# Row gathers without pacing marks in a hybrid decoder block with product-key experts

## The chip, the cores and the metric

One core of a Trainium2 chip runs the whole block in one launch. The metric is device time in microseconds (us) of one execution; the time of a kernel is the median of its runs.

## The reference

The block takes 512 tokens of width 2048. A normalised copy goes through a gated causal convolution and a grouped diagonal state-space model, both are gated, summed, projected and added to the input. Then comes the expert layer, where the stretch of this case lies. In the reference:

```python
s_top, i_top = lax.top_k(s, PEER_TOPK)                 # 8 heads, 2 halves, 128 keys each
best, pos = lax.top_k(cand, PEER_TOPK)                 # cand: sums of pairs
gates = jax.nn.softmax(best, axis=-1)
u_sel, v_sel = u_tab[expert], v_tab[expert]            # tables of 16384 x 2048
act = jax.nn.gelu(jnp.einsum('td,thkd->thk', xb, u_sel))
return jnp.einsum('thk,thkd->td', gates * act, v_sel)
```

So each token takes 8 x 16 = 128 rows of `peer_u`, forms 128 dot products, and adds 128 weighted rows of `peer_v`. A last norm gives the output. All is float32.

## The kernel before

**Two ways through the experts.** Tokens 160 to 511 (352 of them, `ND`) are done densely: all 16384 experts are multiplied on TensorE and the unchosen are masked by a gate of zero. Tokens 0 to 159 (`G0`: a block of `GA` = 128 and one of `GB` = 32) are done by gathering the chosen rows from the tables. The two run side by side in the last 2160 us.

**The dense way.** The 16384 experts are 128 blocks j of 128. `dense_u(j)` multiplies the tokens by one block of `peer_u` (48 matmuls) and applies gelu on ScalarE, which gives `ga`. `weigh(j, ga)` multiplies `ga` by the gates of the block on VectorE (line 987; the gates of `QG` = 4 blocks come in one tile `gq`, which has a single buffer, loaded by `load_gates` on the GpSimd queue) and splits the result in a high part `wh` (ScalarE, line 209) and a low part `wl` (VectorE, line 210). `dense_v(g, dc, ws)` multiplies eight such blocks, group g, by a quarter dc of the columns of `peer_v` (96 matmuls) and adds the result to `acc` on VectorE (`_add`, line 61).

**The loop.** For every group g (16) and quarter dc (4): two new blocks jn go through `dense_u` and `weigh` (from block `LEAD` = 32 on; the first 32 were computed earlier and are read back as `gar`), then `dense_v`. I call one pass of this inner loop a quarter. Quarters of g = 0 to 2 have `dense_v` alone (96 matmuls), those of g = 3 to 14, 48 of them, have all of it (192 matmuls), those of g = 15 have `dense_v` alone again.

**Weights.** Weights are float32 and are used as a high and a low part. `Stream` loads pieces of 512 KB (`wraw`, SyncE's queue), ScalarE makes `whi`, VectorE makes `wlo` (`split`, lines 209 and 210). A piece feeds 24 matmuls; six pieces may be on the way, three of them split. There are four buffers of each part, so the part of a piece can be made once the matmuls of the piece four before it are done, about three pieces ahead of its use. In a quarter of 192 matmuls eight pieces are split.

**The gathered way.** `gather()` is a generator. A step takes one expert for each of 128 partitions: `gather_row` has GpSimd start an indirect DMA of 128 rows of 8 KB (1 MB, tile `grow`), and VectorE does one pass of 128x2048 over it, a dot product for `peer_u` (line 1113) or a weighted sum for `peer_v` (line 1116). There are three buffers (`NROW`), and a gather into a buffer waits for the pass that read it last, three steps before. The steps are 128 + 128 for the first block of tokens and 32 + 32 for the second. `pump_rows(n)` advances the generator; in a full quarter it is called four times with `rate / 2`, after each `weigh`, before and after `dense_v`: 6.1 steps in a quarter.

**Order.** Each engine has one queue and works it in order. A planner lays out the queues when the program is built: it follows the order of the program, but may put an instruction ahead of others that by its own estimate are not ready yet. `with after(x)` ties the instructions of its block on the engine of x behind x in that queue; it adds no wait. In the kernel before, `paced(ap)` has GpSimd copy one column of a tile just made (`ga`, or `acc` after `dense_v`) into a small tile `mark`, and every gather started by `gather_row` is tied behind the latest mark.

Of the kernel before, what the change touches and what calls it, by code (L numbers as in the profile page):

```python
# [7 lines left out]
F32 = mybir.dt.float32  # L8
# [25 lines left out]
NE = 128  # L34
# [121 lines left out]
def kernel(ctx, tc, xT, vecs, cst, w_in, conv_w_out, w_vg, w_out, w_q, keysT,  # L156
# [47 lines left out]
        return pp.tile([128, T], F32, name="ps", tag="proj", bufs=4)  # L204

    pace = [None]

    def split(hi, lo, src, eng=None):
        ins = nc.scalar.copy(hi, src).ins  # L209
        low = (eng or nc.vector).tensor_tensor(lo, src, hi.bitcast(F32), op=ALU.subtract)  # L210
        if eng is nc.gpsimd:
            pace[0] = low.ins
        return ins

    rings = {"raw": [(wp, 4)], "hi": [(wp, 3)], "lo": [(wp, 3)]}
# [763 lines left out]

    def weigh(j, ga):  # L980

        if j % QG == 0:
            load_gates(j // QG)
        if j < LEAD:
            ga = gars.pop(j) if j in gars else reload(j)
        g3 = ga.rearrange("p (b t) -> p b t", t=32)
        nc.vector.tensor_tensor(g3, gq[0][:, :, j % QG, :], g3, op=ALU.mult)  # L987
        p = wgp[j // GRP % 2]
        wh, wl = (p.tile([128, ND], F32R, name=n, tag="w") for n in ("wh", "wl"))
        split(wh, wl, ga)  # L990
        return wh, wl

    def reload(j):
# [60 lines left out]

    def gather_row(tab, ids, e):
        g = row("grow")
        with after(pace[0]):
            nc.gpsimd.indirect_dma_start(out=g, out_offset=None, in_=tab,
                                         in_offset=bass.IndirectOffsetOnAxis(ap=ids[:, e:e + 1], axis=0))
        return g  # L1060

    def gather():
        blocks = [(0, GA, eidx, gta, HK, rt[:, 0:1]),
                  (GA, GB, eidb, gtb, HK // REP, rtb)]
        passes = [(b, tab) for b in blocks for tab in (peer_u, peer_v)]
        todo = [(tab, b[2], e) for b, tab in passes for e in range(b[4])]
        live, xt, gain = [], [], []

        def ahead():
            if todo:  # L1070
                live.append(gather_row(*todo.pop(0)))

        def load(b):
            t0, n = b[:2]
            x = row("xt")
            for c in range(128 // n):
                nc.sync.dma_start(x[c * n:(c + 1) * n], d_xr[t0:t0 + n])
            xt.append(x)

        def load_gain():  # L1080
            gain.append(row("gain"))
            nc.gpsimd.dma_start(gain[0], gffn[None, :].to_broadcast([128, D]))

        def turn(scale):
            x2 = rowp.tile([128, D], F32, name="rows0", tag="rows", bufs=1)
            nc.scalar.activation(x2, xt.pop(), AF.Copy, scale=scale)
            return x2

        load(blocks[0])
        load_gain()  # L1090
        for _ in range(3):
            yield
        for p, (b, tab) in enumerate(passes):
            t0, n, ids, gates, steps, r = b
            nxt = passes[p + 1] if p + 1 < len(passes) else (None, None)
            if tab is peer_u:
                x = turn(r)
                ahead()
                _mul(nc, x, x, gain.pop())
            else:  # L1100
                x = turn(float(n) / 128)
            while len(live) < 2:
                ahead()
            for i in range(steps):
                if i == steps - 2 and nxt[0]:
                    load(nxt[0])
                elif i == steps - 1 and nxt[1] is peer_u:
                    load_gain()
                else:
                    ahead()  # L1110
                g = live.pop(0)
                if tab is peer_u:
                    nc.vector.scalar_tensor_tensor(g, g, 1.0, x, op0=ALU.mult, op1=ALU.mult,  # L1113
                                                   accum_out=act[:, i:i + 1])
                else:
                    nc.vector.scalar_tensor_tensor(x, g, act[:, i:i + 1], x, op0=ALU.mult, op1=ALU.add)  # L1116
                yield
            if tab is peer_u:
                with after(last_ga[0]):
                    nc.scalar.activation(act[:, :steps], act[:, :steps], AF.Gelu_apprx_tanh)  # L1120
                _mul(nc, act[:, :steps], act[:, :steps], gates)
                continue
            if n < 128:
                for _ in range(3):
                    yield
                y = row("ysum")
                for q in range(4):
                    pt = ps_v()
                    nc.tensor.matmul(pt[:n], sel, x[:, q * 512:(q + 1) * 512], start=True, stop=True)  # L1129
                    nc.scalar.copy(y[:n, q * 512:(q + 1) * 512], pt[:n])  # L1130
                x = y
            nc.sync.dma_start(out[t0:t0 + n, :], row_norm(x[:n], gfin))
        yield
# [2 lines left out]
    gth = gather()  # L1136
    gi = [0, 0.0]

    def paced(ap):

        mark = con2.tile([128, 1], F32, name="mark", tag="mark", bufs=2)
        pace[0] = nc.gpsimd.tensor_copy(mark, ap[:, 0:1]).ins  # L1142

    def pump_rows(n):
        gi[1] += n
        while gi[0] < gi[1]:
# [4 lines left out]
    for j in range(LEAD):  # L1151
        if j >= LEAD - 4:
            jn = 2 * (j - LEAD + 4)
            gars.update((i, reload(i)) for i in (jn, jn + 1))
        if j == 0:
            rows_load()
        if j in (4, 6):
            rows_turn()
        ga = dense_u(j, gate_steps if j >= LAG else None)
        if j == LAG - 1:  # L1160
            transp_routes()
        if j >= LEAD - 5:
            paced(ga)
            pump_rows(RLEAD)
        if j >= LEAD - 4:
            ws_next += [weigh(jn, None), weigh(jn + 1, None)]
# [50 lines left out]
    def dense_v(g, dc, ws):  # L1217
        pcs = []
        pairs = [ps_v((2, 512)) for _ in range(2)]
        pvs = [pairs[i // 2][:, i % 2, :ND] for i in range(4)]  # L1220
        last = range(GRP - 2, GRP)
        order = [(e, i) for e in range(GRP - 2) for i in range(4)] + [(e, i) for i in range(4) for e in last]
        for at, (e, i) in enumerate(order):
            if at == 16 and g == NE // GRP - 1 and dc:
                turn_out(dc - 1)
            if e // 2 == len(pcs):
                pcs.append(tabs.take())
            hi, lo = pcs[e // 2]
            wh, wl = ws[e]
            s = slice(e % 2 * 512 + i * 128, e % 2 * 512 + (i + 1) * 128)  # L1230
            nc.tensor.matmul(pvs[i], hi[:, s], wh, start=e == 0, stop=False)  # L1231
            nc.tensor.matmul(pvs[i], hi[:, s], wl, start=False, stop=False)  # L1232
            nc.tensor.matmul(pvs[i], lo[:, s], wh, start=False, stop=e == GRP - 1)  # L1233
        for h in range(2):
            a, pv = acc[:, 4 * dc + 2 * h:4 * dc + 2 * h + 2], pairs[h][:, :, :ND]
            _add(nc, a, pv, a if g else res[dc][:, 2 * h:2 * h + 2])
        paced(acc[:, 4 * dc + 3])
        if g == NE // GRP - 1 and dc == 3:
            turn_out(dc)

# [2 lines left out]
    for g in range(ngrp):  # L1243
        ws = ws_next
        ws_next = []
        for dc in range(4):
            if g == ngrp - 1 and dc == 3:
                for _ in gth:
                    pass
            if g == ngrp - 1 and dc == 0:  # L1250
                hst.close()
                op = ctx.enter_context(tc.tile_pool(name="op", bufs=1, reuse_waits="tile"))
                tail["ost"] = op.tile([128, len(BLKS), D], F32, name="ost")
                tail["sqs"] = op.tile([128, len(BLKS), 4], F32, name="sqs")
                tail["gfb"] = op.tile([128, D], F32, name="gfb")
                nc.gpsimd.dma_start(tail["gfb"], gfin[None, :].to_broadcast([128, D]))
            for jn in range((g + 1) * GRP + 2 * dc, (g + 1) * GRP + 2 * dc + 2):
                if jn < NE:
                    ga = None
                    if jn >= LEAD:  # L1260
                        ga = dense_u(jn)
                        paced(ga)
                    ws_next.append(weigh(jn, ga))
                    if jn >= LEAD:
                        pump_rows(rate / 2)
            n = RV / 4 * (3 + (g > 0)) if (g + 1) * GRP < LEAD else rate / 2 if g < ngrp - 1 else REND / 2 if dc < 3 else 0
            if g == 0 and dc < 3:
                load_res()
            pump_rows(n)
            dense_v(g, dc, ws)  # L1270
            pump_rows(n)
# [83 lines left out]
```

## Time and profile before

| what | value |
| --- | --- |
| median of 3 runs | 3835.49 us (3828.89 to 3838.25) |
| the profiled execution's own time | 3822.91 us |
| its span, from the first to the last instruction | 3821.1 us |
| mean granted TensorE clock | 0.959 |
| TensorE busy with matmuls | 3514.3 us, 92% |
| VectorE busy | 2712.8 us, 71% |
| ScalarE busy | 1256.4 us, 33% |
| GpSimd busy | 1004.8 us, 26% |
| moved by DMA | 852.35 MB, mean 223 GB/s |

The busy shares are means over the whole span, whose stages differ: up to about 1480 us the projections, convolution, state space and routing run, then the first 32 blocks of `dense_u`, and from 1661 us the loop. PEclk is the clock that TensorE was granted as a share of full speed. A DMA share is the mean busy share of the core's 16 DMA engines. Idle time is put down to the engine or transfer whose signal ended it.

### The profile page before, as it was taken

The page shows a single profiled execution, that of the slowest core. Times are in us where ns is not written, and L with a number is a line of the kernel's source. Part 1 is how long each engine was busy: PE and PEld are TensorE (multiplying, and loading weights), DVE is VectorE, ACT ScalarE, POOL GpSimd, SP SyncE. Part 2 cuts the span into 40 slices and gives each one's busy share as a digit, 9 for nine tenths or more (in the row PEclk, how much of TensorE's full clock was granted, in tenths as well). Part 3 has the DMA queues.
Part 4 walks back from the last instruction along what each step waited for, and adds up shares of the span by engine and source line. Part 5 has one row for each costly group of instructions (what it writes and reads, how often), then busy time and mean ns, then how long its engine had stood idle before and what let it go on. Part 6 is the DMA issues. An engine that isn't in the chain of part 4 may idle for free. (4 is left out here: it accounts for less than half of the span.)

```text
span 3821.1 us, 49889 instructions
## 1 busy us (share of the span) xinstructions
PE 3514.3 (92%) x19059; PEld 3257.5 (85%) x19059; DVE 2712.8 (71%) x4006; ACT 1256.4 (33%) x2009; POOL 1004.8 (26%) x832
## 2 busy tenths in 40 slices
PE   8999999999999999989998998988788888889877
PEld 6888888888888899988998998888788887889877
DVE  8686678985349998756667677676576666767666
ACT  4334434242323348732222222232222222232223
POOL 1100001000025452121233233333343333332331
PEclk9999999999999999999999999999899999999988
DMA  5533444344444356687678888886788767888874
GB/s 184 140 109 115 127 126 143 114 133 140 141 136 121 116 165 208 224 304 254 236 289 301 302 304 306 302 305 245 262 299 292 283 248 267 300 303 308 313 274 182
DMA packets 218863, 852.35 MB, mean 223 GB/s; under 512 B 41168, under 2 KB 58656, under 8 KB 173376
## 3 DMA queue, kind: packets, MB, share of 16 engines
q1 hardware_dynamic: 144704, 437.58, 35.8%
q0 software_dynamic: 64512, 396.12, 27.3%
q10 hardware_dynamic: 9408, 15.47, 1.1%
q8 instruction: 149, 2.44, 0.3%
q14 instruction: 90, 0.74, 0.1%
HBM read 795.23 MB, written 53.84 MB: 222 GB/s over the span
## 5 line engine op out<-in xcount | busy, mean ns | idle before, releaser
L209 ACT CAST whi<-wraw 128x1024 fp32r<-128x1024 f32 x736 | 761.6, 1049 | 1462.4 <-PE ps L269 575.0
L210 DVE TENSOR_TENSOR wlo<-wraw,whi 128x1024 fp32r<-128x1024 f32 x682 | 830.6, 1225 | 227.1 <-ACT whi L209 226.7
L1233 PE MATMUL pv<-wh,wlo 128*128 128x352 f32 x2048 | 707.2, 345 | 178.3 <-DVE wlo L210 178.2
L1231 PE MATMUL pv<-wh,whi 128*128 128x352 f32 x2048 | 704.4, 344 | 34.8 <-DVE acc L61 32.8
L270 PE MATMUL pu<-h2h,wlo 128*128 128x352 f32 x2048 | 676.0, 330 | 50.8 <-DVE wlo L210 50.8
L1232 PE MATMUL pv<-wl,whi 128*128 128x352 f32 x2048 | 696.5, 340 | 0.0
L268 PE MATMUL pu<-h2l,whi 128*128 128x352 f32 x2048 | 681.1, 333 | 1.1 <-ACT whi L209 1.1
L269 PE MATMUL pu<-h2h,whi 128*128 128x352 f32 x2048 | 668.2, 326 | 0.0
L1116 DVE SCALAR_TENSOR_TENSOR rows<-grow,act,rows 128x2048 f32<-128x2048 f32 x160 | 375.7, 2348 | 332.2 <-DMA grow<-in_peer_v_dram,eidx 282.1
L1233 PEld LDWEIGHTS pv<-wh,wlo 128*128 128x128 f32 x2048 | 417.8, 204 | 194.3 <-DVE wlo L210 194.3
L1113 DVE SCALAR_TENSOR_TENSOR grow<-grow,rows 128x2048 f32<-128x2048 f32 x160 | 366.2, 2289 | 277.3 <-DMA grow<-in_peer_u_dram,eidx 227.4
L1231 PEld LDWEIGHTS pv<-wh,whi 128*128 128x128 f32 x2048 | 418.3, 204 | 39.2 <-DVE acc L61 36.0
L270 PEld LDWEIGHTS pu<-h2h,wlo 128*128 128x128 f32 x2048 | 390.7, 191 | 58.1 <-DVE wlo L210 58.0
L1232 PEld LDWEIGHTS pv<-wl,whi 128*128 128x128 f32 x2048 | 419.0, 205 | 0.0
L268 PEld LDWEIGHTS pu<-h2l,whi 128*128 128x128 f32 x2048 | 393.3, 192 | 1.4 <-ACT whi L209 1.4
L269 PEld LDWEIGHTS pu<-h2h,whi 128*128 128x128 f32 x2048 | 391.8, 191 | 0.0
L268 PE MATMUL ps<-hl,whi 128*128 128x512 f32 x896 | 353.2, 394 | 8.7 <-ACT whi L209 8.7
L270 PE MATMUL ps<-hh,wlo 128*128 128x512 f32 x896 | 350.7, 392 | 0.5 <-DVE wlo L210 0.4
L269 PE MATMUL ps<-hh,whi 128*128 128x512 f32 x896 | 350.2, 391 | 0.0
L209 ACT CAST wh<-ga 128x352 fp32r<-128x352 f32 x96 | 46.7, 486 | 834.7 <-DVE ga L987 834.7
L1142 POOL COPY mark<-acc 128x1 f32<-128x1 f32 x64 | 84.5, 1320 | 757.2 <-DVE acc L61 757.2
L1142 POOL COPY mark<-ga 128x1 f32<-128x1 f32 x101 | 97.5, 966 | 506.5 <-ACT ga L916 492.4
(347 smaller groups left out, 5134.0 us busy)
## 6 DMA issues: line engine op xcount, KB each, us to landing
wraw<-in_peer_ut_dram SPq DMA_DIRECT2D x256, 512.0 KB
wraw<-in_peer_vt_dram SPq DMA_DIRECT2D x256, 512.0 KB
wraw<-in_w_in_dram SPq DMA_DIRECT2D x112, 512.0 KB
d_g<-stg SPq DMA_DIRECT2D x22, 1024.0 KB
gq<-d_g POOLq DMA_DIRECT2D x32, 704.0 KB, 11.1
wraw<-in_w_vg_dram SPq DMA_DIRECT2D x32, 512.0 KB
wraw<-in_w_out_dram SPq DMA_DIRECT2D x32, 512.0 KB
wraw<-in_w_q_dram SPq DMA_DIRECT2D x32, 512.0 KB
```

The costliest lines, as they stand in the source:

```text
L209: ins = nc.scalar.copy(hi, src).ins
L210: low = (eng or nc.vector).tensor_tensor(lo, src, hi.bitcast(F32), op=ALU.subtract)
L268: nc.tensor.matmul(ps, hi[:, sl], al[k], start=k == 0, stop=False)
L269: nc.tensor.matmul(ps, hi[:, sl], ah[k], start=False, stop=False)
L270: nc.tensor.matmul(ps, lo[:, sl], ah[k], start=False, stop=k == nk - 1)
L1113: nc.vector.scalar_tensor_tensor(g, g, 1.0, x, op0=ALU.mult, op1=ALU.mult, accum_out=act[:, i:i + 1])
L1116: nc.vector.scalar_tensor_tensor(x, g, act[:, i:i + 1], x, op0=ALU.mult, op1=ALU.add)
L1142: pace[0] = nc.gpsimd.tensor_copy(mark, ap[:, 0:1]).ins
L1231: nc.tensor.matmul(pvs[i], hi[:, s], wh, start=e == 0, stop=False)
L1232: nc.tensor.matmul(pvs[i], hi[:, s], wl, start=False, stop=False)
L1233: nc.tensor.matmul(pvs[i], lo[:, s], wh, start=False, stop=e == GRP - 1)
```

## The change

Three edits. The marks go, with `paced`, and the gathers are no longer tied to anything: each waits only for its buffer and its indices. VectorE's pass over a row is tied behind the low part that VectorE was last given in the order of the program (`last_low`, kept by `split`). And the gates of a group of four blocks are loaded after the last block of the group before has been weighed, rather than just ahead of their first use.

```diff
+    last_low = [None]
...
         if eng is nc.gpsimd:
             pace[0] = low.ins
+        else:
+            last_low[0] = low.ins
...
-        if j % QG == 0:
-            load_gates(j // QG)
+        if j == 0:
+            load_gates(0)
...
         split(wh, wl, ga)
+        if j % QG == QG - 1 and j + 1 < NE:
+            load_gates(j // QG + 1)
...
         g = row("grow")
-        with after(pace[0]):
-            nc.gpsimd.indirect_dma_start(out=g, out_offset=None, in_=tab,
-                                         in_offset=bass.IndirectOffsetOnAxis(ap=ids[:, e:e + 1], axis=0))
+        nc.gpsimd.indirect_dma_start(out=g, out_offset=None, in_=tab,
+                                     in_offset=bass.IndirectOffsetOnAxis(ap=ids[:, e:e + 1], axis=0))
...
-                if tab is peer_u:
-                    nc.vector.scalar_tensor_tensor(g, g, 1.0, x, op0=ALU.mult, op1=ALU.mult,
-                                                   accum_out=act[:, i:i + 1])
-                else:
-                    nc.vector.scalar_tensor_tensor(x, g, act[:, i:i + 1], x, op0=ALU.mult, op1=ALU.add)
+                with after(last_low[0]):
+                    if tab is peer_u:
+                        nc.vector.scalar_tensor_tensor(g, g, 1.0, x, op0=ALU.mult, op1=ALU.mult,
+                                                       accum_out=act[:, i:i + 1])
+                    else:
+                        nc.vector.scalar_tensor_tensor(x, g, act[:, i:i + 1], x, op0=ALU.mult, op1=ALU.add)
...
-    def paced(ap):
-
-        mark = con2.tile([128, 1], F32, name="mark", tag="mark", bufs=2)
-        pace[0] = nc.gpsimd.tensor_copy(mark, ap[:, 0:1]).ins
...
         if j >= LEAD - 5:
-            paced(ga)
             pump_rows(RLEAD)
...
-        paced(acc[:, 4 * dc + 3])
...
                         ga = dense_u(jn)
-                        paced(ga)
                     ws_next.append(weigh(jn, ga))
```

## Rows read from the trace of the kernel before

**Rows 1.** The page: busy time, share of the span, instructions.
```profile
PE   3514.3 (92%) x19059; PEld 3257.5 (85%) x19059; DVE 2712.8 (71%) x4006; ACT 1256.4 (33%) x2009; POOL 1004.8 (26%) x832
```

**Rows 2.** Waits from 1886.9 to 3712 us: total, times, longest.
```profile
DVE rows L1116 <- DMA grow<-in_peer_v_dram,eidx: 282.1, 47, 9.9
...
PE pv L1233 <- DVE wlo L210: 177.1, 51, 6.2
...
DVE grow L1113 <- DMA grow<-in_peer_u_dram,eidx: 187.7, 46, 9.6
...
PE pu L270 <- DVE wlo L210: 46.5, 22, 5.4
```

**Rows 3.** Stages and single quarters: engines' busy time (instructions), clock, DMA share, GB/s.
```profile
1660.90:1886.90 226.00, 200.87 (x1155) 196.93 (x1155) 145.36 (x165) 63.95 (x78) 39.92 (x38) 0.94 0.77 267
1886.90:1917.80 30.90, 30.90 (x193) 30.90 (x192) 20.88 (x21) 9.73 (x13) 13.12 (x9) 1.00 0.83 305
2063.60:2101.00 37.40, 33.54 (x194) 33.26 (x193) 27.58 (x30) 9.69 (x13) 11.90 (x10) 0.91 0.75 285
1886.90:3712.00 1825.10, 1601.48 (x9217) 1579.75 (x9216) 1256.10 (x1107) 474.69 (x587) 628.63 (x461) 0.93 0.80 290
3712.00:3821.00 109.00, 76.34 (x441) 71.23 (x439) 68.26 (x83) 31.61 (x54) 19.26 (x15) 0.87 0.51 192
...
1799.20:1814.70 15.50, 15.50 (x98) 15.50 (x97) 10.05 (x11) 5.93 (x9) 3.27 (x3) 1.00 0.87 308
```

**Rows 4.** VectorE's timeline in one quarter: start, duration, instruction, idle before.
```profile
2061.53 2.29 DVE L1113 SCALAR_TENSOR_TENSOR grow<-grow,rows 128x2048 f32<-128x2048 f32 x1 [1.91 <-DMA grow<-in_peer_u_dram,eidx]
...
2069.60 2.29 DVE L1113 SCALAR_TENSOR_TENSOR grow<-grow,rows 128x2048 f32<-128x2048 f32 x1
...
2083.33 2.29 DVE L1113 SCALAR_TENSOR_TENSOR grow<-grow,rows 128x2048 f32<-128x2048 f32 x1 [8.36 <-DMA grow<-in_peer_u_dram,eidx]
...
2085.98 1.22 DVE L210 TENSOR_TENSOR wlo<-wraw,whi 128x1024 fp32r<-128x1024 f32 x1
```

**Rows 5.** GpSimd's timeline in the same quarter.
```profile
2072.84 1.04 POOL L1142 COPY mark<-acc 128x1 f32<-128x1 f32 x1 [12.40 <-DVE acc L61]
2074.03 1.77 POOL L1058 DMA_INDIRECT grow<-in_peer_u_dram,eidx  x1 [0.16 <-issue]
...
2077.41 0.97 POOL L1058 DMA_INDIRECT grow<-in_peer_u_dram,eidx  x1 [0.15 <-issue]
```

**Rows 6.** TensorE's timeline in the same quarter.
```profile
2087.26 0.66 PE L1233 MATMUL pv<-wh,wlo 128*128 128x352 f32 x1 [3.86 <-DVE wlo L210]
```

**Rows 7.** Line 1058: issue time on GpSimd (ns min/median/max), issue to landing.
```profile
L1058 POOL DMA_INDIRECT grow<-in_peer_v_dram,eidx x128: 941/970/4914, 2547.5 to 3364.6; - x128
...
DMA to landing us min/median/max: 5.3/9.4/15.1
```

**Rows 8.** Around 3405 to 3433 us: GpSimd, VectorE, then two stretches.
```profile
3413.46 1.71 POOL L1058 DMA_INDIRECT grow<-in_peer_u_dram,eidb  x1 [2.63 <-DVE grow L1113]
...
3421.51 2.29 DVE L1113 SCALAR_TENSOR_TENSOR grow<-grow,rows 128x2048 f32<-128x2048 f32 x1 [0.75 <-DMA grow<-in_peer_u_dram,eidb]
...
3400.00:3500.00 100.00, 91.46 (x542) 89.54 (x541) 78.66 (x79) 28.71 (x36) 35.58 (x30) 0.97 0.90 336
...
3405.00:3433.00 28.00, 23.72 (x142) 22.56 (x142) 24.80 (x23) 5.80 (x7) 12.67 (x10) 1.00 1.00 379
```

**Rows 9.** Waits from 1660.9 to 1886.9 us.
```profile
PE pv L1231 <- DVE acc L61: 22.0, 9, 4.2
...
DVE gar L987 <- DMA gq<-d_g: 8.3, 3, 5.4
```

**Rows 10.** Waits from 3712 us to the end.
```profile
DVE rows L1116 <- DMA grow<-in_peer_v_dram,eidb: 15.5, 5, 7.6
...
PE pv L1231 <- DVE acc L61: 10.9, 2, 9.6
...
PE pv L1201 <- DVE acc L61: 7.4, 2, 6.7
```

## The prediction

> **What bounds the kernel now.** I read the busy shares first: TensorE is busy 92% of the span and VectorE 71% [rows 1]. That looks like a kernel at TensorE's limit, with no more than 8% to gain. So the second view is what TensorE's idle time waits for, in the loop alone. In the 48 full quarters it waits for one thing, VectorE's low parts: 177.1 us ahead of the third matmul of `dense_v` and 46.5 us ahead of that of `dense_u` [rows 2]. The two add up to 223.6 us, which is all of its idle time there, 1825.1 - 1601.5 [rows 3]. And VectorE is not short of time: 1256.1 us of 1825.1 [rows 3]. In the same stretch it stands still for rows of the first block of tokens, 282.1 us ahead of line 1116 and 187.7 us ahead of line 1113 [rows 2], and what is queued behind the pass that waits is low parts.
>
> The timelines of one quarter (2063.6 to 2101) show the chain. VectorE comes to a pass at 2074.97 and waits 8.36 us for its row; the low part that TensorE needs comes behind it, at 2085.98 [rows 4]; TensorE stood idle for 3.86 us until then [rows 6], its whole idle time in that quarter, 37.40 - 33.54 [rows 3]. Why was the row late? Its buffer is the one that the pass at 2061.53 had read, free at 2063.82 [rows 4]. Its gather began at 2074.03, 10.2 us later, behind a mark that had waited 12.40 us for `acc` [rows 5]. The third gather of the burst is late too: buffer free at 2071.89 [rows 4], begun at 2077.41 [rows 5]. So the limit of this stage is a late start of a transfer that takes 9.4 us from issue to landing, in the median [rows 7].
>
> A quarter without these waits exists: 1886.9 to 1917.8, 193 matmuls in 30.9 us with no idle, at clock 1.00; the mean of the 48 is 1825.1 / 48 = 38.0 us [rows 3]. Of the 7.1 us between them 223.6 / 48 = 4.7 are idle; the other 2.4 are busy time, (1601.5 / 48) - 30.9: the mean clock is 0.93, and it is below 1.00 where there was idle time, 0.91 in the quarter above against 1.00 in the clean one [rows 3]. The two levels are 2.4 and 1.2 GHz, so some matmuls after a stall run at half speed.
>
> **The change part by part.** *The gathers.* Each now starts when the pass three steps before has ended. The stretch of 3405 to 3433 already holds some: the gather at 3413.46 was released by VectorE's pass and not by a mark, and its row was consumed at 3421.51 after a wait of 0.75 us [rows 8]. Compared with rows 5 a gather gains between 5.5 and 10.2 us of lead. How long a wait costs nothing? In rows 4 and 6 a wait of 8.36 us cost 3.86 us, so about 4.5 us are covered, by the low parts being made some three pieces ahead. A wait of 8.36 us less at least 5.5 of lead is 2.9 us, under the cover. So I expect TensorE's idle time in the full quarters to go, and the slow clock with it.
>
> What is late next? First TensorE itself, 30.9 us. Then the DMA engines. A quarter moves 290 GB/s x 38.0 us = 11.0 MB [rows 3]. Over 28 us with chasing gathers they moved 379 GB/s at a share of 1.00, which is 29.1 us a quarter; the 100 us around it had 336 GB/s at a share of 0.90, which is 32.8 us [rows 8]. A ring of three buffers gives a row every (9.4 + 0.3 + 2.29) / 3 = 4.0 us (the 0.3 is an estimate for the signal to GpSimd, twice its 0.16 of issue [rows 5]), 24.4 us for 6.1 rows, so it does not bind at that landing time. VectorE's work in the worked quarter is 27.6 us [rows 3], under 30.9 but not by much. So a quarter lies between 30.9 and 32.8 us. I take 32.0, a little nearer to the DMA end, because a share of 1.00 says that transfers will wait for one another wherever gathers chase. That is 48 x (38.0 - 32.0) = 288 us less; at the ends 341 and 250.
>
> *First stage, 226.0 us.* Twelve quarters of `dense_v` alone; a clean one takes 15.5 [rows 3], so 186 is the floor and 40 the most to win. The idle is 22.0 us for `acc` [rows 9], adds that stand behind waiting passes. I take 25 (the idle, and a little clock); bounds 0 and 40.
>
> *Tail, 109 us.* TensorE waits 10.9 and 7.4 us for `acc`, VectorE 15.5 us for rows [rows 10]. The last rows chase already and the closing norm stays. I take 10; bounds 0 and 22.
>
> *The marks.* 1.04 us of GpSimd and a wait of 12.40 [rows 5], on an engine that nothing else waits for; their removal alone is 0, covered by GpSimd's idle time.
>
> *The tie.* It adds no wait. It keeps a pass from being queued ahead of a low part that the program has first. Behind a pass that still waits stand the next low parts, the adds to `acc`, and TensorE behind those; the cover is the 4.5 us. Without that cover each us of waiting would cost one.
>
> *The gates.* `gq` has one buffer, so its load can begin no sooner than the fourth multiply of the group before, as now. It may gain the 8.3 us that VectorE waits for it in the first stage [rows 9]. It may also lose: on GpSimd's queue it waits for that multiply, and a gather queued behind it waits too, at most the 7.7 us of one block (half of 15.5); less the cover that is 3.2 us in every second quarter, 77 us. The planner puts what is ready first, so I take 0 and keep -8 and +77.
>
> Sum: 288 + 25 + 10 = 323 us off the profiled execution's own 3822.9 (a span of 3821.1 and 1.8 around it) gives 3500. The median of the runs lies a factor of 1.0033 above that execution, so the forecast is **3511 us**.
>
> One rule speaks against the change. The issue of a gather took 0.97 us in the median and up to 4.91 [rows 7]. The Trainium skill ("SBUF — State Buffer", section "SBUF: two separate sides") says that descriptors of DMAs from GpSimd's queue are written by its cores, which are locked out while VectorE runs certain two-port operations. Gathers that start right behind a pass start beside VectorE's low parts; were each issue 4.91 us by that rule, the ring would give (9.4 + 3.9 + 0.3 + 2.29) / 3 = 5.3 us a row and 32.3 us a quarter, some 15 us over my sum. The issue at 3413.46 took 1.71 us [rows 8], so the trace bears it out in part.
>
> **The rivals.** *Landing gets late (half the gain or less).* With the DMA engines full, a landing could take the longest seen, 15.1 us [rows 7]. The ring then gives (15.1 + 0.3 + 2.29) / 3 = 5.9 us a row, 36.0 us a quarter: 48 x 2.0 = 96 off, with half of the other terms 113, so 3710 and by the factor 3722. For it: the share of 1.00 [rows 8]. Against it: bursts of three are what the transfers queue behind now, and they go. It decides from a landing of 12.6 us on, where three rows take 3 x 30.9 / 6.1.
>
> *A clump (slower).* The program asks for three rows in succession after the second `weigh`, and the tie only says what a pass follows, not what follows it. If the planner, without marks, lines up four passes with no low part between, the fourth has its gather begun at the end of the first (2.3 us), landed at 2.3 + 0.3 + 9.4 = 12.0, and is reached at 6.9: a wait of 5.1, and low parts blocked for 4 x 2.29 + 5.1 = 14.3 us. In rows 4 a block of 8.36 + 2.29 = 10.7 us cost 3.86, so 6.8 are covered; 7.5 us idle, and 2.4 for the clock, make a quarter of 40.8: 48 x 2.8 = 134 us more, 3957, by the factor 3970. It decides from a block of 11.5 us, where idle reaches 4.7. Against it: the low parts of `dense_v` come between the third pass and the next, and VectorE now queues passes and low parts by turns.
>
> *It does not do what it says.* The gathers may keep their place, if GpSimd's queue puts them behind a gate load or if passes are queued as late as now. Then 3835, within 0.3%.
>
> **How the numbers follow.** Forecast 3511: 0.63. Late landing, 3722: 0.16. No effect: 0.06. Clump, 3970: 0.15. The forecast's own terms reach from 3822.9 - 341 - 40 - 22 - 8 = 3412, by the factor 3423, to 3822.9 - 250 + 77 = 3650, by the factor 3662. All terms at their best at once are unlikely, so the range begins at 3430; it ends at 3725 to take in the late landing. Faster by more than 0.3%, about what a measurement of this kernel can tell from none, 0.63 + 0.16 = 0.79; same 0.06; slower 0.15.
>
> **What would show it.** Right: gathers on GpSimd released by VectorE's passes, within half a us of their end; waits for rows in the full quarters down from 470 us to below 150; TensorE's wait for low parts from 224 us to below 50; clock above 0.98; a quarter near 32 us at some 345 GB/s. Wrong on size: idle gone, but DMA share at 1.00 and landings above 12.6 us. Wrong altogether: a wait ahead of every fourth pass, or gathers behind a gate load, with TensorE's wait for low parts as long as now.

## The result, and the profile after

The changed kernel takes **3483.6 us** in the median of four runs (3476.6 to 3483.9); the kernel before, on the same chip, 3832.2. The ratio is 0.9091 with a 95% interval of 0.9062 to 0.9121. The forecast was 3511, so the time is 27 us below it and inside the range. The profiled execution took 3476.6 us, with a span of 3474.6.

First the page of the changed kernel, which answers [rows 1] (busy time, share of the span, instructions):

```profile
PE 3387.5 (97%) x19059; PEld 3152.7 (91%) x19059; DVE 2716.9 (78%) x4006; ACT 1273.5 (37%) x2009; POOL 859.7 (25%) x667
```

TensorE went from 92% to 97% with the same 19059 instructions; VectorE did the same work in a shorter span. Where the time went is read from the stages, which answer [rows 3]: the stretch ahead of the loop, the first stage, the 48 full quarters, one clean quarter, the two quarters at the change of token block, the tail (columns as in [rows 3]).

```profile
1400.00:1674.00 274.00, 268.49 (x1862) 266.49 (x1863) 188.59 (x239) 182.47 (x495) 69.50 (x55) 0.98 0.65 218
1674.00:1883.40 209.40, 192.28 (x1156) 190.53 (x1155) 139.74 (x160) 63.44 (x78) 30.64 (x25) 0.97 0.79 276
1883.40:3380.00 1496.60, 1487.48 (x9218) 1485.52 (x9217) 1271.93 (x1115) 492.81 (x587) 500.19 (x317) 1.00 0.94 354
2053.00:2083.90 30.90, 30.90 (x193) 30.90 (x193) 26.16 (x27) 10.11 (x12) 11.28 (x8) 1.00 0.98 374
3095.70:3171.40 75.70, 66.58 (x386) 64.62 (x385) 58.75 (x60) 24.41 (x30) 24.57 (x17) 0.95 0.94 352
3380.00:3474.60 94.60, 74.31 (x441) 69.52 (x439) 62.98 (x79) 31.49 (x54) 13.05 (x9) 0.91 0.52 197
```

| stage | before | after | forecast | measured |
|---|---|---|---|---|
| ahead of the loop | 1660.9 | 1674.0 | 0 | +13.1 |
| first stage | 226.0 | 209.4 | -25 | -16.6 |
| 48 full quarters | 1825.1 | 1496.6 | -288 | -328.5 |
| tail | 109.0 | 94.6 | -10 | -14.4 |

The full quarters carry nearly all of it. TensorE's idle time in them fell from 223.6 to 1496.6 - 1487.5 = 9.1 us and the clock rose from 0.93 to 1.00; 46 of the 48 are as clean as the one of 2053 to 2083.9. The waits of 1883.4 to 3380 answer [rows 2] (total, times, longest):

```profile
POOL grow L1062 <- DVE grow L1118: 472.1, 108, 14.5
POOL grow L1062 <- DVE rows L1121: 452.1, 140, 10.1
...
DVE rows L1121 <- DMA grow<-in_peer_v_dram,eidx: 53.7, 40, 3.7
DVE grow L1118 <- DMA grow<-in_peer_u_dram,eidx: 40.3, 26, 2.8
...
PE pv L1232 <- DVE wlo L211: 5.2, 2, 3.4
```

The line numbers are a few off those of before: the passes are now 1118 and 1121, the gather 1062. VectorE's waits for rows of the first block fell from 469.8 to 94.0 us, and TensorE's wait for low parts ahead of the third matmul of `dense_v` from 177.1 to 5.2. The waiting moved to GpSimd: 248 of its gathers now wait for a pass. One quarter on GpSimd (first fence) and VectorE (second), as in [rows 5] and [rows 4]:

```profile
2059.35 2.77 POOL L1062 DMA_INDIRECT grow<-in_peer_u_dram,eidx  x1 [2.14 <-DVE grow L1118]
...
2071.70 0.94 POOL L1062 DMA_INDIRECT grow<-in_peer_u_dram,eidx  x1 [4.74 <-DVE grow L1118]
```

```profile
2056.78 2.28 DVE L1118 SCALAR_TENSOR_TENSOR grow<-grow,rows 128x2048 f32<-128x2048 f32 x1
...
2062.71 2.29 DVE L1118 SCALAR_TENSOR_TENSOR grow<-grow,rows 128x2048 f32<-128x2048 f32 x1 [1.43 <-DMA grow<-in_peer_u_dram,eidx]
...
2064.93 3.49 DVE L211 TENSOR_TENSOR wlo<-wraw,whi 128x1024 fp32r<-128x1024 f32 x3
2068.34 0.88 DVE L61 TENSOR_TENSOR acc<-pv,acc 128x704 f32<-128x704 f32 x1
2069.14 2.28 DVE L1118 SCALAR_TENSOR_TENSOR grow<-grow,rows 128x2048 f32<-128x2048 f32 x1
2071.35 0.88 DVE L61 TENSOR_TENSOR acc<-pv,acc 128x704 f32<-128x704 f32 x1
```

The pass at 2056.78 ends at 2059.06 and the gather into its buffer begins at 2059.35; the one at 2069.14 ends at 2071.42, its gather begins at 2071.70. In [rows 4, 5] the same step took 10.2 us. The order on VectorE changed too: three low parts stand in one piece at 2064.93. In the quarter of [rows 4] they stood one by one between the passes:

```profile
2063.74 1.22 DVE L210 TENSOR_TENSOR wlo<-wraw,whi 128x1024 fp32r<-128x1024 f32 x1
2065.45 2.29 DVE L1113 SCALAR_TENSOR_TENSOR grow<-grow,rows 128x2048 f32<-128x2048 f32 x1 [0.49 <-DMA grow<-in_peer_u_dram,eidx]
...
2067.67 1.22 DVE L210 TENSOR_TENSOR wlo<-wraw,whi 128x1024 fp32r<-128x1024 f32 x1
```

That second difference turned out to matter as much as the first.

### The profile page after: what moved, and what is told of

Read it like the earlier page. It is cut to its first block, busy times and chain, and to the rows that moved or that the text cites. A ratio compares the mean times of both kernels' runs of the same rounds, so it can differ in the third digit from the quotient of the medians.

```text
span 3474.6 us, 49596 instructions
## 1 busy us (share of the span) xinstructions
PE 3387.5 (97%) x19059; PEld 3152.7 (91%) x19059; DVE 2716.9 (78%) x4006; ACT 1273.5 (37%) x2009; POOL 859.7 (25%) x667
## 5 line engine op out<-in xcount | busy, mean ns | idle before, releaser
L273 PE MATMUL pu<-h2h,wlo 128*128 128x352 f32 x2048 | 664.0, 324 | 24.4 <-POOL wlo L211 20.1
L1230 PE MATMUL pv<-wh,whi 128*128 128x352 f32 x2048 | 669.7, 327 | 16.2 <-DVE acc L61 15.8
L1232 PE MATMUL pv<-wh,wlo 128*128 128x352 f32 x2048 | 663.6, 324 | 7.0 <-DVE wlo L211 6.9
L1231 PE MATMUL pv<-wl,whi 128*128 128x352 f32 x2048 | 661.4, 323 | 0.0
L1230 PEld LDWEIGHTS pv<-wh,whi 128*128 128x128 f32 x2048 | 387.1, 189 | 18.8 <-DVE acc L61 17.3
L1232 PEld LDWEIGHTS pv<-wh,wlo 128*128 128x128 f32 x2048 | 387.1, 189 | 8.2 <-DVE wlo L211 8.2
L1231 PEld LDWEIGHTS pv<-wl,whi 128*128 128x128 f32 x2048 | 389.5, 190 | 0.0
L1062 POOL DMA_INDIRECT grow<-in_peer_u_dram,eidx x128 | 200.3, 1565 | 527.6 <-DVE grow L1118 480.8
L1062 POOL DMA_INDIRECT grow<-in_peer_v_dram,eidx x128 | 208.9, 1632 | 416.8 <-DVE rows L1121 391.7
L271 PEld LDWEIGHTS ps<-hl,whi 128*128 128x128 f32 x896 | 168.9, 188 | 46.0 <-ACT whi L210 9.5
```

The lines of the kernel that those rows point to most:

```text
L271: nc.tensor.matmul(ps, hi[:, sl], al[k], start=k == 0, stop=False)
L273: nc.tensor.matmul(ps, lo[:, sl], ah[k], start=False, stop=k == nk - 1)
```

## The experiments

Theory at the start, from the prediction: all of the gain comes from the earlier start of the gathers; the tie and the early gate loads are worth nothing. Rival: the tie carries it.

**Gathers put back behind their marks, tie and early gates kept.**

```diff
-        nc.gpsimd.indirect_dma_start(out=g, ...)
+        with after(pace[0]):
+            nc.gpsimd.indirect_dma_start(out=g, ...)
...
+            paced(ga)
...
+        paced(acc[:, 4 * dc + 3])
```

> The changed kernel with the gathers alone put back: each follows its mark again, while the tie and the early gate loads stay. Theory (all of the gain comes from the earlier start of the gathers): back at the kernel before, 3800 to 3850 us, with TensorE's wait for low parts in the full quarters near 220 us and VectorE's waits for rows near 470 us. Rival (the tie carries the gain, by keeping passes that wait from standing ahead of low parts): under 3700 us, with the waits for rows as long as before and TensorE's wait for low parts under 100 us.

Measured: 3577.4 us (3574.7 to 3583.4), ratio 0.9337 (0.9300 to 0.9373). The full quarters, and VectorE's waits for rows of the first block from 1890 to 3470 us:

```profile
1879.30:3476.30 1597.00, 1523.79 (x9217) 1513.26 (x9216) 1278.58 (x1114) 483.63 (x587) 631.87 (x461) 0.98 0.88 332
```

```profile
DVE rows L1122 <- DMA grow<-in_peer_v_dram,eidx: 114.7, 83, 6.9
...
DVE grow L1119 <- DMA grow<-in_peer_u_dram,eidx: 84.6, 39, 5.0
```

With the marks back, 252 us of the gain stayed; the theory that the gathers carry it alone falls. The rival's time came, and so did TensorE's short wait: all its idle time there is 73 us. Its mechanism did not: the waits for rows did not stay as long as before, they fell from 469.8 to 199 us.

**Tie taken away.**

```diff
-                with after(last_low[0]):
+                if True:
```

> The changed kernel without the tie: the passes are no longer held behind the low parts that the program has before them; gathers without marks and early gate loads stay. Theory: within 1% of the changed kernel's 3484 us (3450 to 3520), since a row that has landed makes a pass 2.29 us long wherever it stands. Rival (the tie is what stops a clump): passes line up ahead of low parts, TensorE's wait for low parts in the full quarters is above 100 us, and the time is 3600 us or more.

Measured: 3635.4 us (3625.6 to 3641.5), ratio 0.9479 (0.9439 to 0.9519). The tie is worth 152 us on top of the free gathers. The rival's time came, but not its sign: TensorE's whole idle time in the full quarters is 87 us (1610.3 less 1523.0), under the 100 that it named. What the time goes into is read from the run with the gathers alone, below.

**The other three of the eight combinations.** Each is the kernel before with one edit. (All three also note the last low part in `last_low`; only the tie uses it.) The gathers alone:

```diff
-        with after(pace[0]):
-            nc.gpsimd.indirect_dma_start(out=g, ...)
+        nc.gpsimd.indirect_dma_start(out=g, ...)
...
-            paced(ga)
...
-        paced(acc[:, 4 * dc + 3])
```

> The kernel before with nothing changed but the gathers: no marks, no tie, gates loaded at the old place. Theory formed from the two runs before this one (the tie is what now paces the passes; without marks and without tie nothing does): passes run ahead of their place in the program, 8 or more a quarter instead of 6.1, until the list of rows or a buffer holds them; quarters with 8 passes take about 35 us and quarters without any 30.9, so 3600 to 3660 us, like the kernel without the tie (3635). Theory of the prediction (the earlier start of the gathers carries the gain by itself): 3470 to 3520 us.

Measured: 3638.2 us (3637.1 to 3641.9), ratio 0.9498 (0.9468 to 0.9528), as the first theory said. The tie alone:

```diff
-                if tab is peer_u:
+                with after(last_low[0]):
+                    if tab is peer_u:
```

> The kernel before with nothing added but the tie: gathers behind their marks, gates loaded at the old place. Theory (the tie puts the passes at places from which the marks follow sooner, so it alone gives most of the gain, and the early gate loads nothing): as the run with marks, tie and early gates, 3565 to 3595 us, and the time from the end of a pass to the start of the gather into its buffer is near 1 us in the median instead of 5.6. Rival (the early gate loads carried that run): above 3700 us.

Measured: 3573.8 us (3560.2 to 3574.9), ratio 0.9317 (0.9282 to 0.9351), as expected. The median time from the end of a pass to the start of the gather into its buffer was 1.12 us. The early gate loads alone:

```diff
-        if j % QG == 0:
-            load_gates(j // QG)
+        if j == 0:
+            load_gates(0)
...
+        if j % QG == QG - 1 and j + 1 < NE:
+            load_gates(j // QG + 1)
```

> The kernel before with nothing added but the early gate loads: gathers behind their marks, no tie. Theory (one buffer holds the load back to where it was): 3820 to 3850 us. Rival (the early gate loads help when gathers follow marks): under 3700 us. Rival (a gate load that waits for its multiply holds the gathers behind it): above 3870 us.

Measured: 3887.9 us (3882.4 to 3894.1), ratio 1.0153 (1.0120 to 1.0185): 1.5% slower.

**Gates at the old place, gathers and tie kept.**

```diff
-        if j == 0:
-            load_gates(0)
+        if j % QG == 0:
+            load_gates(j // QG)
...
-        if j % QG == QG - 1 and j + 1 < NE:
-            load_gates(j // QG + 1)
```

> The changed kernel with the gate loads back at the first multiply of their group; gathers without marks and the tie stay. Theory (the early load is worth nothing in the full quarters, since one buffer holds it back): 3475 to 3495 us, with VectorE's waits for gq in the first stage between 8 and 20 us. Rival A (the early load keeps gathers waiting on GpSimd's queue): up to 77 us faster, 3407 us. Rival B (the early load is needed): 3500 us or more, with waits for gq in the full quarters.

Measured: 3488.7 us (3481.7 to 3489.0), ratio 0.9095 (0.9060 to 0.9130), the changed kernel's within the intervals. VectorE's waits for `gq` in the first stage were 13.1 us in three, to the tenth those of the changed kernel. Together:

| gathers | tie | gates | median us |
|---|---|---|---|
| - | - | - | 3829 |
| - | - | early | 3888 |
| - | tie | - | 3574 |
| - | tie | early | 3577 |
| free | - | - | 3638 |
| free | - | early | 3635 |
| free | tie | - | 3489 |
| free | tie | early | 3484 |

(The first line is the kernel before beside these runs; it lay between 3828.6 and 3833.9 on the chips used.) The tie alone gives 255 us, the free gathers alone 191, both 340: they overlap by 106, so they work in part on the same thing. The early gate loads are worth nothing beside either, and cost 59 us without them.

What is that thing? For every row of the full quarters I took the gather's start less the end of the pass three before it, which frees its buffer (a count over the starts in the traces), and its median: before 5.60 us; early gates alone 5.60; tie alone 1.12; tie and early gates 1.12; all kernels with free gathers 0.28. The tie alone shortens it because it moves the passes, not the gathers. From the kernel with the tie alone, GpSimd and then VectorE:

```profile
2210.88 2.11 POOL L1146 COPY mark<-acc 128x1 f32<-128x1 f32 x1 [9.95 <-DVE acc L61]
2213.15 1.78 POOL L1061 DMA_INDIRECT grow<-in_peer_u_dram,eidx  x1 [0.16 <-issue]
```

```profile
2207.65 2.28 DVE L1117 SCALAR_TENSOR_TENSOR grow<-grow,rows 128x2048 f32<-128x2048 f32 x1
...
2210.66 2.29 DVE L1117 SCALAR_TENSOR_TENSOR grow<-grow,rows 128x2048 f32<-128x2048 f32 x1
...
2212.87 3.50 DVE L211 TENSOR_TENSOR wlo<-wraw,whi 128x1024 fp32r<-128x1024 f32 x3
```

The mark still waits 9.95 us for `acc`, but the passes now stand beside the adds to `acc`, so a buffer is free (2209.93 and 2212.95) only just before the gather (2213.15), and while the row travels VectorE makes three low parts. In [rows 4] the pass stood 10 us ahead of its gather and the next one was in the way of the low part. In the waits of the full quarters 141 gathers of this kernel are released by a pass, against 47 before:

```profile
POOL grow L1061 <- DVE rows L1120: 188.8, 76, 7.0
POOL grow L1061 <- DVE grow L1117: 166.3, 65, 5.7
```

**Two rows under way instead of three**, tie kept. This takes the lead away again and leaves the order of the tie.

```diff
-        nc.gpsimd.indirect_dma_start(out=g, ...)
+        with after(pace[0]):
+            nc.gpsimd.indirect_dma_start(out=g, ...)
...
-                else:
-                    ahead()
                 g = live.pop(0)
...
+                if i < steps - 2 or ...:
+                    paced(act[:, i:i + 1] if tab is peer_u else x)
+                    ahead()
                 yield
```

> The changed kernel with two rows under way instead of three: a gather is asked for after the pass that it follows by two, not by three, and a small copy on GpSimd that reads that pass's result holds it until then. Ring theory with the landing of 9.4 us from the kernel before: (9.4 + 0.6 + 2.3) / 2 = 6.2 us a row, 37.5 us for 6.05 rows, 48 x 6.3 = 302 us more, about 3785 us. With a landing of 7.3 us, the shortest time from a gather's start to its pass in the changed kernel: 5.1 us a row, 30.9 us a quarter, nearly no loss, 3485 to 3530 us. Rival (rows have slack to spare and the third buffer is worth nothing): within 10 us of the changed kernel.

Measured: 3819.1 us (3810.6 to 3832.6), ratio 0.9969 (0.9949 to 0.9988). With the tie in place and a later gather (7.44 us in the median after the buffer is free) the whole gain but 0.3% is gone. Its full quarters:

```profile
1887.60:3703.30 1815.70, 1588.84 (x9218) 1552.12 (x9218) 1272.21 (x1111) 477.29 (x587) 651.96 (x600) 0.95 0.82 290
```

1815.7 / 48 = 37.8 us a quarter, where the expected ring gave 37.5. The ring is the cause, but two of its terms were off and nearly cancel. By the starts in this trace a gather began 1.34 us in the median after the pass that it follows, not 0.6. And 216 of the 289 passes waited for their row; these began 8.6 us in the median after their gather's start, not 9.4. The means of all rows add up: (8.8 + 1.4 + 2.3) / 2 = 6.25 us a row, and the passes came every 6.26.

So the order of the tie, without the lead of the gathers, does not keep the gain. What the tie would be worth at the old lead is not shown: here a gather began later after its buffer was free than before, 7.44 against 5.60 us.

**Why free gathers without the tie stop at 3638.** The marks were also what kept the passes to their pace. VectorE's passes on the first table in the kernel with the gathers alone (two records each), in the stages after the first:

```profile
1926.20:2338.40 412.20, 204.09 (x178) 0.97 0.96 368
2338.40:2554.20 215.80, 0.00 (x0) 1.00 0.57 186
```

The first stretch is 12 quarters. The 89 passes fall into the first 11 of them, 8.1 a quarter, and then for over 200 us there is none, until the Gelu on `act`, which has an order of its own behind the `ga` of its place in the program, runs at 2509.16. In the changed kernel 163 records in 416.6 us are 81.5 passes in 13.5 quarters, 6.0 each:

```profile
1883.40:2300.00 416.60, 184.56 (x163) 1.00 0.91 348
```

All engines in the same two stretches of the kernel with the gathers alone:

```profile
1926.20:2338.40 412.20, 381.61 (x2307) 377.20 (x2306) 351.06 (x349) 117.84 (x146) 140.69 (x96) 0.97 0.96 368
2338.40:2585.10 246.70, 246.70 (x1538) 246.70 (x1537) 144.32 (x129) 80.33 (x98) 31.14 (x22) 1.00 0.63 210
```

The crowded stretch loses 30.6 us of TensorE (VectorE 85% busy, DMA at 0.96) and the empty one cannot give it back, since TensorE was already at its limit. The same comes again in the 20 quarters that follow, with the passes on the second table, 35 us a quarter:

```profile
2585.00:3284.00 699.00, 644.87 (x3845) 636.88 (x3844) 583.50 (x466) 201.59 (x248) 227.15 (x155) 0.96 0.95 357
```

In all the full quarters take 1607.3 us here, 110.7 more than in the changed kernel. The profiled execution is 161 us longer; 42.8 of them are lost ahead of the full quarters, which begin at 1926.2 and not at 1883.4, and where 39 passes run and not 19: they ran ahead there too. Whether VectorE or the DMA engines set the crowded quarters is not told apart.

**More bytes beside the rows.** I had taken 1.1 us a quarter for crowded DMA engines. First with the loads on SyncE's queue:

```diff
             pump_rows(n)
+            if 3 <= g < ngrp - 1:
+                for q in range(4):
+                    nc.sync.dma_start(xtra, peer_v[q * 128:(q + 1) * 128, dc * 512:(dc + 1) * 512])
             dense_v(g, dc, ws)
```

> The changed kernel with 1 MB more of loads in each of the 48 full quarters: four 256 KB pieces of a table into a spare tile that nothing reads. A quarter then moves about 12.6 MB instead of 11.6. Theory A (the DMA engines still have room beside TensorE's 30.9 us): within 15 us of the changed kernel, 3470 to 3500 us. Theory B (379 GB/s, the highest that a stretch of 28 us showed before, is all they give): 12.6 MB take 33.3 us, 48 x 2.4 = 115 us more, about 3600 us, with rows and weights waited for on VectorE and ScalarE.

Measured: 3543.3 us, ratio 0.9254 (0.9224 to 0.9284), and no answer: the loads depend on nothing, so they were issued between 1121.8 and 1947.4 us, ahead of the stage they were meant for. The full quarters were left as they were (1495.6 us); they began 64 us later. So the loads were tied to their quarter:

```diff
                     ws_next.append(weigh(jn, ga))
+                    if 3 <= g:
+                        nc.scalar.copy(xtra[:, 0:1], ws_next[-1][0][:, 0:1].bitcast(F32))
+                        nc.scalar.dma_start(xtra, peer_v[jn * 128:(jn + 1) * 128, :896])
```

> The changed kernel with two more loads in each full quarter, each of 448 KB into a spare tile that nothing reads, issued from ScalarE's queue right behind the high part of a multiplied tile, so that they stay in their quarter. That is 0.92 MB more beside the 11.0 MB of a quarter (354 GB/s x 31.0 us). Theory A (the DMA engines have room left beside TensorE's 30.9 us): within 15 us of the changed kernel, 3470 to 3500 us. Theory B (the 368 GB/s of the stretch with 8 passes a quarter in the kernel with the gathers alone is what they give): 11.9 MB take 32.3 us, 48 x 1.4 = 67 us more, about 3550 us, with longer waits for rows on VectorE.

Measured: 3511.5 us (3509.6 to 3514.6), ratio 0.9153 (0.9131 to 0.9175), 28 us over the changed kernel: between the two theories. Its full quarters, and the densest 400 us:

```profile
1891.80:3413.80 1522.00, 1498.08 (x9218) 1489.56 (x9217) 1271.59 (x1115) 509.68 (x683) 482.58 (x317) 0.99 0.98 376
```

```profile
2240.00:2640.00 400.00, 396.61 (x2453) 393.88 (x2452) 333.63 (x299) 134.89 (x182) 119.94 (x84) 1.00 0.99 378
```

31.7 us a quarter, 0.5 more, with 8% more bytes, at 376 GB/s. Of the 33 us between the two profiled executions that is 25; the other 8 were lost ahead of the full quarters. VectorE's waits for rows, of both blocks, rose from 112 to 165 us. So the rows come later near 378 GB/s and a share of 0.99; the changed kernel, at 354 and 0.94, is below that. It is not shown that all of the 0.5 us is the DMA engines': ScalarE, whose queue issued the loads, stood 55.7 us for earlier loads into the spare tile.

**What the changed kernel still loses.** Ahead of the loop, GpSimd and TensorE:

```profile
1398.78 0.99 POOL L1062 DMA_INDIRECT grow<-in_peer_u_dram,eidx  x1 [24.75 <-DVE eidx L860]
1399.80 2.35 POOL L211 TENSOR_TENSOR wlo<-wraw,whi 128x1024 fp32r<-128x1024 f32 x1
```

```profile
PE pu L273 <- POOL wlo L211: 20.1, 1, 20.1
```

Without a mark to follow, the first gather was put at the head of GpSimd's queue before its indices were there, and the low part that TensorE needed stood behind it for 24.75 us. Keeping `with after(pace[0])` around the gather, without any marks, puts it behind GpSimd's last low part or gate step instead:

```diff
-        nc.gpsimd.indirect_dma_start(out=g, ...)
+        with after(pace[0]):
+            nc.gpsimd.indirect_dma_start(out=g, ...)
```

> The changed kernel with each gather put behind the last low part or gate step that GpSimd was given in program order; no marks, and the tie and the early gate loads stay. In the changed kernel the first gather stood on GpSimd's queue 24.75 us before its indices were there, GpSimd's low part waited behind it, and TensorE 20.1 us for that. Theory (this wait is all that the changed kernel lost ahead of its loop, and the gathers in the loop are not touched): 13 to 20 us faster than the changed kernel, 3464 to 3471 us, with full quarters still near 31.2 us. Rival (another wait takes its place, for the indices are late anyway): within 5 us of the changed kernel.

Measured: 3472.9 us (3466.9 to 3473.9), ratio 0.9061 (0.9027 to 0.9095). The row of 20.1 us is gone and the loop begins at 1665.9 instead of 1674.2: 8.3 us. That is less than the 13 to 20 expected of the whole time: it began at 1660.9 before, so 5.0 us are still lost. By the intervals alone this is not apart from the changed kernel.

The second loss is the 75.7 us of two quarters at the change of block. On top of the edit above, six empty steps stand there in the list of rows:

```diff
             while len(live) < 2:
                 ahead()
+            if p == 2:
+                for _ in range(6):
+                    yield
...
-    steps_g = 2 * HK + 2 * HK // REP + 7
+    steps_g = 2 * HK + 2 * HK // REP + 13
```

> The changed kernel with the gathers put behind GpSimd's last low part or gate step in program order (as in the run that did this alone) and with six empty steps in the list of rows at the change of token block, where two quarters took 42.1 and 34.8 us. Theory (the rows asked for while the closing norm still holds their buffers come late, and low parts stand behind them): the two quarters fall to 31 to 36 us each, 5 to 15 us less than that run, 3455 to 3468 us. Rival (the norm's own waits hold the low parts): the two quarters stay near 77 us together and the time within 3 us of 3473.

Measured: **3457.9 us** (3452.6 to 3459.7, five runs), ratio 0.9005 (0.8986 to 0.9024), below the changed kernel's interval, and the fastest of all. Its 48 full quarters:

```profile
1879.80:3363.70 1483.90, 1482.97 (x9218) 1482.68 (x9217) 1270.03 (x1114) 493.32 (x587) 507.66 (x317) 1.00 0.94 356
```

30.9 us each, idle time 0.9 us in all: TensorE is the limit there.

## Why the prediction was right, and where it was not

**What bounds the kernel, and where it would stop: right.** Late rows stood ahead of low parts, TensorE waited for these, the clock fell after the waits; with the rows in time a quarter is TensorE's 30.9 us. The signs came as named: gathers 0.28 us behind a pass, waits for rows under 150 us, TensorE's wait for low parts under 50, clock 1.00, 31.2 us a quarter at 354 GB/s. That the lead of the gathers is what counts is shown by the run with two rows under way.

**The tie at 0: wrong.** This is the step that failed. That the time came out right all the same was luck in the split: the prediction gave everything to the gathers, and its sum held because the tie was made with them. I looked for what the tie adds ("it adds no wait") and not for what it moves. It puts passes behind low parts and beside the adds, so that with the old marks the buffer-to-gather time falls from 5.60 to 1.12 us: 255 us by itself. And without marks it is the only thing that keeps 6 passes a quarter; I priced the removal of the marks at 0 on GpSimd's time, but a mark also paces.

**The gathers at -323: too much credit.** Alone they give 191 us. The failing step is "each now starts when the pass three steps before has ended": true, but it took VectorE's order of passes as given, and the order follows the gathers.

**The gates at 0: right beside the tie or the free gathers** (3489 and 3484; 3574 and 3577; 3638 and 3635). With marks and no tie they cost 59 us, inside my -8 to +77; why is open: TensorE's waits for low parts rise by 36 us (171.8 + 87.5 against 223.6), while the waits for rows hardly change.

**The DMA term: too large by 0.8 us a quarter.** I took 32.0 between 30.9 and 32.8 and got 31.2, of which 0.3 are the two quarters at the change of block. The 336 GB/s at a share of 0.90 in [rows 8] was no limit but a stretch with waits in it; the 379 at 1.00 is about what the run with more bytes reached, 378. 11.0 MB at 378 GB/s are 29.2 us, under TensorE's 30.9, so the lower end of the quarter, 341 us off, was the one to take; 328.5 came, less by the two quarters at the change of block.

**First stage and tail: sizes off, inside their bounds.** 16.6 instead of 25: the waits for `acc` fell from 22.0 to 15.1 us only, and those for `gq` rose from 8.3 to 13.1. 14.4 instead of 10 in the tail.

**Ahead of the loop: not foreseen.** 13.1 us more, of which the run that mends it gives 8.3 back. I had asked of each moved step what queue it stands in, but not of the first gathers, which lost the mark that kept them behind GpSimd's low parts. GpSimd was to me "an engine that nothing else waits for"; that holds in the full quarters, but ahead of the loop TensorE waited 20.1 us for a low part that GpSimd makes.

**The rivals.** Late landing did not come. The changed kernel's trace has no landings of rows, but that of the run with `after(pace[0])` alone has all of them, with the same 0.28 us from pass to gather: 5.6 us at the least, 9.3 in the median and 13.2 at the most in the full quarters. The rival decided only from 12.6 on. The clump came in another form, and only without the tie: not four passes in succession but some 8 a quarter for 11 and then for 20 quarters, and even that was faster than before.

**The rule that spoke against the change** came true in small. The issues of gathers rose from 0.97 us in the median [rows 7] to 1.68 on the same table, because more of them now begin beside VectorE's work:

```profile
L1062 POOL DMA_INDIRECT grow<-in_peer_v_dram,eidx x128: 937/1677/2927, 2437.7 to 3078.8; - x128
```

The Trainium skill ("SBUF — State Buffer", section "SBUF: two separate sides") names such a lock-out; the trace agrees in direction. By what VectorE was doing at the start of each of the 291 gathers in the full quarters (a count over the trace), the median issue took 0.94 us with VectorE idle (25 gathers), 0.94 beside an add to `acc`, which reads PSUM (45), 1.68 beside a low part (162) and 2.75 beside a pass on the first table's rows (34). Before, 139 of 291 began beside an idle VectorE and took 0.95. But no issue took longer than 2.99 us, and with rows every 5.1 us (30.9 / 6.05) a ring of three has room for that.

## What to carry to other kernels

An order imposed on instructions is to be priced by what it moves, not only by the waits that it adds, and one that is taken away by what it paced, at its first use too. Where a transfer is late, two numbers of the trace say most: the time from the moment its buffer is free to the moment it is asked for, and how many of its consumers fall into one stage. A total that comes out right does not show which part of a change did it; the parts have to be run one by one.

## What the runs showed of the hardware

The DMA engines carried row gathers and weight tiles together at 376 GB/s over 1522 us, at a share of 0.98, and a quarter took 0.5 us longer in that run; in the changed kernel a clean quarter of 374 GB/s at 0.98 cost TensorE nothing. The issue of a row gather from GpSimd took 0.94 us beside an idle VectorE or an add from PSUM, 1.68 beside a low part and 2.75 beside a pass. Loads with nothing to wait for were issued 800 us and more early on SyncE's queue (from 1121.8 us on, for quarters that began at 1947.7), so an experiment that adds traffic has to tie it to its place.
